# Transposes of probabilities and of v in two row halves of 64, with a PSUM bank for each half

## The chip, the cores and the metric

The kernel runs on one core of a Trainium2 chip. The metric is the time of one execution on the device in microseconds (us). The chip's engines go by these names: PE is TensorE's matrix product and PEld its loading of the stationary operand ("weights"), DVE is VectorE, ACT is ScalarE, POOL is GpSimd, SP is SyncE, which here only issues transfers. Each engine works through its own queue in order and waits on semaphores for the others. PSUM, into which PE writes, has eight banks of 512 fp32 values for each of 128 partitions.

## The reference

One decoder layer over 1024 prompt tokens and 8 x 4 decode tokens, all in fp32. What matters here is the sliding-window attention of the prompt, 8 heads of 64 on 2 key/value heads, in blocks of 128 queries that see their own block and the one before:

```python
def _sink_attention(q, k, v, mask, sinks):
    s = jnp.einsum('bnqhgd,bnkhd->bnhgqk', q, k) * (HEAD_DIM ** -0.5)
    s = jnp.where(mask, s, -jnp.inf)
    m = jnp.maximum(jnp.max(s, axis=-1, keepdims=True), sink)
    p = jnp.exp(s - m)
    denom = jnp.sum(p, axis=-1, keepdims=True) + jnp.exp(sink - m)
    return jnp.einsum('bnhgqk,bnkhd->bnqhgd', p / denom, v)
```

Around it stand an RMS norm and one input projection (q, k, v and a pooling branch), a pooling mixer, one output projection over both branches, a second norm, a SwiGLU network of width 2816, and a gated per-layer input:

```python
    x = x + _rms(mix, n_mix_post)
    f = _rms(x, n_ffn_pre)
    f = (silu(f @ w_gate) * (f @ w_up)) @ w_down
    x = x + _rms(f, n_ffn_post)
    x = x + sigmoid(x @ w_ple_gate) * (p @ w_ple)
```

## The kernel before, in words

Activations lie with the channels on the partitions and the 1056 tokens along the free dimension, in three groups of 352 tokens (`G`, `N`). Large products are made of a high and a low fp32r part for each operand, three matmuls for each chunk of 128 input channels (`gemm`, through the helper `mm`, L128). A weight tile arrives by DMA and is split in two: a cast on ACT (L173) gives the high part, a subtraction on DVE (L174) the low part.

Attention works on the eight blocks of 128 queries in the order 6, 7, 5, 0, 1, 2, 3, 4; in what follows "the second block" is the second in this order. For one block, `scores` multiplies q and k of both key/value heads in two row halves of the PE array (64 channels each) and merges the scores of the current and the previous block into one tile of 128 keys for each head: a key column that lies after the query belongs to the previous block. `weigh` makes the softmax: maxima, exponentials (ACT, L732), sums and reciprocals (DVE, L737 and L738), and a multiplication on POOL (L740). The rows of the tile are queries, its columns keys.

`turned` transposes the eight heads with PE, so that the keys lie on the partitions. A transpose is a matmul through the helper `mt` (L122): the data are the stationary operand, the identity is the moving one. Four heads go into one PSUM bank, and two multiplications by 0/1 masks on DVE take them out: `ptc` (L796) for the keys of the current block, `ptp` (L798) for those of the previous block. `values` multiplies with v in two query halves of 64, because the merged tile lets a half be served by `vmix`, in which rows 64 to 127 come from the block before:

```python
        for i, v in enumerate((vmix, vtok)):
            for kv, cols, hs in sides:
                mm(os_[i][cols, :256], v[:, b, cols], ptc[:, hs, q[i]], start=True, stop=False)
        for i in range(2):
            for kv, cols, hs in sides:
                mm(os_[i][cols, :256], vtok[q[i], b - 1, cols], ptp[q[i], hs, q[i]], start=False, stop=True)
```

`v_turned`, ahead of the eight blocks, transposes v in the same way; ACT copies it to `vtok` (L690), and POOL copies to `vmix` (L691, L692).

Between the steps of a block stand products of the output projection, which `filler` takes from a list (`out_pool`, `out_attn`, `out_proj`): the loop runs scores of the next block, one fill product, transposes, one fill product, values. PE's own order is the written one (`keep_in_program_order` in `mt` and `mm`). On the other engines a scheduler may reorder, except for the instructions that pass through `fix` while `fixed[0]` is set, which is so in the last block and in some other places.

After attention, `ffn_steps` begins with the RMS norm of the output projection (`rstd_steps`): sums over the partitions on PE, a square root on ACT (L395), a reciprocal on DVE (L396), two diagonal matrices on DVE (L402), and their product with a tile of ones on PE, which spreads the result over all partitions. Meanwhile `out_attn` goes on and adds its products to the sum in SBUF (L908).

Of the kernel before, what the change touches and what calls it, by code (L numbers as in the profile page):

```python
# [13 lines left out]
ALU = mybir.AluOpType  # L14
AX = mybir.AxisListType

P = 128
# [14 lines left out]
WIN = 128  # L32
NB = SEQ // WIN
# [5 lines left out]
REST = FFC - SLAB * NSLAB  # L39

AHEAD = 3

LOOK = 4
PLE = 256
# [18 lines left out]
def trunk_kernel(  # L63
# [33 lines left out]
    te, ve, se, ge = nc.tensor, nc.vector, nc.scalar, nc.gpsimd  # L97
# [10 lines left out]
    def nm(s):  # L108
        cnt[0] += 1
        return f"{s}{cnt[0]}"  # L110

    def act_tile(shape, dt=F32, s="a"):
        return apool.tile(shape, dt, tag="a", bufs=A_SLOTS, name=nm(s))
# [3 lines left out]

    pinned = [False]

    def mt(out, src):  # L120

        ins = te.transpose(out, src, ident)  # L122
        if pinned[0]:
            tc.keep_in_program_order(ins)

# [6 lines left out]
    def bank():  # L132
        return psum.tile([P, 512], F32, tag="b", name=nm("b"))
# [4 lines left out]
    def const(shape, src=None, s="c", dt=F32):  # L138
        t = cpool.tile(shape, dt, name=nm(s))
        if src is not None:  # L140
            nc.scalar.dma_start(t, src)
        return t
# [3 lines left out]
    ident = const([P, P])  # L146
# [20 lines left out]
    def fix(ins):  # L167

        if fixed[0]:
            tc.keep_in_program_order(ins)  # L170
# [75 lines left out]
    def step(kind, *args):  # L246
        STEPS.append((kind, args))

    def s_one(s, i):
        c = SLAB * s + i  # L250
        step("one", s, i, (direct_item(w_gu[c, 0]), direct_item(w_gu[c, 1])))
# [5 lines left out]
    def s_dn_one(s, *ts):  # L257
        for t in ts:
            step("dn_one", s, t, direct_item(w_dn[s, t // 2, t % 2]))
# [4 lines left out]
    def s_dn_rest(*gs):  # L264
        step("dn_rest", gs, [direct_item(w_dl[j], (P, REST, 512)) for j in range(2)])

    for s in range(AHEAD):
        for i in range(SLAB):
# [4 lines left out]
    for s in range(NSLAB):  # L273
        for i in range(SLAB):
            s_pair(s, i)
            if s == 0 and i < 2:
                s_dn_one(AHEAD - 1, 2 * i, 2 * i + 1)
                if i == 1:
# [8 lines left out]
    step("combine")  # L287
    for s in range(AHEAD, NSLAB):
        for i in range(SLAB):
            s_one(s, i)  # L290
            if s > AHEAD:
                s_dn_one(s - 1, i)
            if (s, i) == (AHEAD, 1):
                s_dn_rest(0, 1)
# [367 lines left out]
    kT, vT, qT = qkv[0], qkv[1], qkv[2:]  # L662
# [5 lines left out]
    qd, am, vdec = misc[:, 0, :], misc[:, 1:5, :], misc[: NDEC * DSEQ, 5, :]  # L668
# [12 lines left out]
    vtok, vmix = act_tile([P, NB, P]), act_tile([P, NB, P])  # L681

    def v_turned():
        for h in range(2):
            ps = bank()
            for i in range(4):
                b = 4 * h + i
                mt(ps[:, i * P : (i + 1) * P], vT[:, b * P : (b + 1) * P])
            v = ps.rearrange("p (b c) -> p b c", c=P)
            se.copy(vtok[:, 4 * h : 4 * h + 4, :], v)  # L690
            ge.tensor_copy(vmix[0:64, 4 * h : 4 * h + 4, :], vtok[0:64, 4 * h : 4 * h + 4, :])  # L691
        ge.tensor_copy(vmix[64:P, 1:NB, :], vtok[64:P, 0 : NB - 1, :])  # L692
        ps = bank()
        mt(ps[: NDEC * DSEQ, :P], vT[:, SEQ:])
        se.copy(vdec, ps[: NDEC * DSEQ, :P])
        nc.scalar.dma_start(kp_o, kT[:, SEQ - WIN : SEQ])
        nc.scalar.dma_start(vp_o, vtok[:, NB - 1, :])
# [44 lines left out]
    def m4(i):  # L742
        return am[:, i, :].unsqueeze(1).to_broadcast([P, 4, WIN])

    def v4(a):
        return a.rearrange("p (c k) -> p c k", k=WIN)

    def scores(b, now_=True):


        t = act_tile([P, 8, WIN])
        nk = 2 * WIN if b else WIN
        lo = b * WIN + WIN - nk
        at = WIN * 4 // nk
        both = [[bank() for _ in range(4 // at)] for _ in range(2)]
        for c in range(4):
            for kv in range(2):
                rows = slice(64 * kv, 64 * kv + 64)
                i = c % at
                mm(  # L760
                    both[kv][c // at][:, i * nk : (i + 1) * nk],
                    qT[c][rows, b * WIN : (b + 1) * WIN],
                    kT[rows, lo : lo + nk],
                    start=True,
                    stop=True,
                )
        for kv in range(2):
            tk = t[:, 4 * kv : 4 * kv + 4, :]
            for i, ps in enumerate(both[kv]):
                tc_ = tk[:, i * at : (i + 1) * at, :]  # L770
                v = ps.rearrange("p (c k) -> p c k", k=nk)
                if b:
                    m = am[:, 0, :].unsqueeze(1).to_broadcast([P, at, WIN])
                    se.copy(tc_, v[:, :, :WIN])
                    ve.copy_predicated(tc_, m.bitcast(mybir.dt.int32), v[:, :, WIN:])
                else:
                    ve.tensor_tensor(tc_, v, m4(1), op=ALU.add)
        if now_:
            weigh(t)
        return t  # L780
# [6 lines left out]
    def turned(b, t):  # L787

        ptc = act_tile([P, 8, WIN])
        ptp = act_tile([P, 8, WIN]) if b else None  # L790
        for kv in range(2):
            ps = bank()
            hs = slice(4 * kv, 4 * kv + 4)
            for c in range(4):
                mt(ps[:, c * P : (c + 1) * P], t[:, 4 * kv + c, :])
            fix(ve.tensor_tensor(ptc[:, hs, :], v4(ps), m4(2), op=ALU.mult))  # L796
            if b:
                fix(ve.tensor_tensor(ptp[:, hs, :], v4(ps), m4(3), op=ALU.mult))  # L798
        return ptc, ptp

    def values(b, parts):
# [132 lines left out]

    order = [6, 7, 5, 0, 1, 2, 3, 4]
    v_turned()
    fixed[0] = True
    td = dscores()
    fixed[0] = False
    t = scores(order[0], False)  # L940
# [15 lines left out]
    for a, b in zip(order, order[1:] + [None]):  # L956

        fixed[0] = lazy[0] = b is None
        t2 = ahead or (None if b is None else scores(b))
        ahead = None  # L960
        filler(1)
        parts = turned(a, t)
        if b is None:
            lazy[0] = False
            weights(WOA[1][0], 1)
        filler(1)
        values(a, parts)
        t = t2
# [251 lines left out]
    def do_one(s, i, items):  # L1220
        if (s, i) == (AHEAD, 0):
            do_reload_sums()
        sl = tmp(N, "sl")
        se.activation(sl, direct(need(items[0]), fs[2]), AF.Silu)
        ve.tensor_tensor(sl, sl, direct(need(items[1]), fs[2]), op=ALU.mult)
        hid_put(2, s, i, sl)
# [85 lines left out]
    def do_reload_sums():  # L1312
        os_[2] = [half(2, s="o") for _ in range(2)]
        for d, t in zip(osd, os_[2]):
            nc.sync.dma_start(t, d)
# [217 lines left out]
```

## Time and profile before

| | |
|---|---|
| median of 3 runs | 1080.22 us (1079.08 to 1080.45) |
| profiled execution | 1079.83 us, of which the span from its first to its last instruction is 1078.0 us |
| PE busy, PEld busy | 1071.1 us (99%), 1052.5 us (98%) |
| DVE, ACT, POOL busy | 874.9 us (81%), 510.7 us (47%), 277.4 us (26%) |
| granted TensorE clock | 1.0 |
| HBM | 113.86 MB read, 15.87 MB written |
| transposes of v | at 128.2 us of the span |
| transposes of the eight blocks | from 147.8 to 212.4 us |
| feed-forward and gated input | from about 216 us to the end |

All times in rows of the trace are counted from the start of the span. In a row of the time line stand the start, the time, the engine, the line, the operation, output<-input by the program's names, for PE the part of the array (rows * columns), the shape, and the count of like instructions that the row holds; its time then reaches from the start of the first to the end of the last. In brackets stands idle time ahead of it and what ended it. Matmuls are pipelined: the time of one includes its way through the array, so the distance of two starts tells what one costs. `128*128` uses the whole array; `64*128` means that two products stand in the row halves at the same time.

### The profile page before, as it was taken

To read this page: it belongs to the slowest core of one execution; us is meant where nothing else is said; L and a number is where in the kernel's file an instruction comes from. 1 tells how busy PE (TensorE), PEld (TensorE's weight loads), DVE (VectorE), ACT (ScalarE), POOL (GpSimd) and SP (SyncE) were. 2 spreads that over 40 slices of the span, in tenths; PEclk is the share of its full clock that TensorE was granted. 3 is DMA by queue.
4 is the path that set the end of the run, shared out by engine and by line. 5 is a ranking of instruction groups with operands and counts; after the bars stand their busy time and mean duration, and the time that the engine had idled before them with its cause. 6 is when DMAs were issued, how large, how long until landed. Compare 5 with 4: busy or idle time off the path is not lost. (4 is left out here: it accounts for less than half of the span.)

```text
span 1078.0 us, 17744 instructions
## 1 busy us (share of the span) xinstructions
PE 1071.1 (99%) x6883; PEld 1052.5 (98%) x6883; DVE 874.9 (81%) x1303; ACT 510.7 (47%) x872; POOL 277.4 (26%) x211
## 2 busy tenths in 40 slices
PE   9999999999999999999999999999999999999998
PEld 9999988899999999999999999999999999999998
DVE  6876378896979967796598898898899998969983
ACT  7423277664555533445543343343344365545441
POOL 0073022200000024445445444444452000023300
PEclk9999999999999999999999999999999999999999
DMA  8121311543544422322212212212234556454361
GB/s 299 59 73 40 104 53 40 201 152 135 215 165 137 138 98 78 135 76 79 89 70 82 92 62 90 87 59 98 79 113 167 176 176 248 157 212 151 107 207 61
DMA packets 43572, 130.88 MB, mean 121 GB/s; under 512 B 5060, under 2 KB 15716, under 8 KB 43488
## 3 DMA queue, kind: packets, MB, share of 16 engines
q1 hardware_dynamic: 42160, 127.98, 34.5%
q10 hardware_dynamic: 1328, 1.77, 0.5%
q8 instruction: 54, 0.88, 0.3%
q14 instruction: 30, 0.25, 0.1%
HBM read 113.86 MB, written 15.87 MB: 120 GB/s over the span
## 5 line engine op out<-in xcount | busy, mean ns | idle before, releaser
L1104 POOL TENSOR_TENSOR wr<-wr,wr 128x512 f32<-128x512 f32 x108 | 171.0, 1597 | 480.2 <-DMA wr<-in_w_gu_dram 257.0
L173 ACT CAST wh<-wr 128x1024 fp32r<-128x1024 f32 (+1 forms) x138 | 142.1, 1031 | 166.0 <-PE b L128 104.2
L174 DVE TENSOR_TENSOR wl<-wr,wh 128x1024 fp32r<-128x1024 f32 (+1 forms) x138 | 169.0, 1226 | 43.2 <-ACT wh L173 24.6
L128 PE MATMUL b<-fh,wh 128*128 128x352 f32 x624 | 201.7, 323 | 0.6 <-DVE p L1131 0.6
L128 PE MATMUL b<-fl,wh 128*128 128x352 f32 x624 | 199.8, 320 | 0.0
L128 PE MATMUL b<-fh,wl 128*128 128x352 f32 x624 | 199.7, 320 | 0.0
L173 ACT CAST sh<-wr 128x1024 fp32r<-128x1024 f32 x72 | 75.7, 1052 | 138.3 <-POOL wr L1104 123.1
L128 PE MATMUL b<-fh,sh 128*128 128x352 f32 x416 | 134.3, 323 | 0.0
L128 PE MATMUL b<-fl,sh 128*128 128x352 f32 x416 | 133.2, 320 | 0.0
L128 PE MATMUL b<-fh,sl 128*128 128x352 f32 x416 | 133.1, 320 | 0.0
L174 DVE TENSOR_TENSOR sl<-wr,sh 128x1024 fp32r<-128x1024 f32 x72 | 98.6, 1370 | 37.9 <-ACT sh L173 20.1
L128 PEld LDWEIGHTS b<-fh,wh 128*128 128x128 f32 x624 | 117.0, 187 | 1.3 <-DVE p L1131 0.9
L128 PEld LDWEIGHTS b<-fl,wh 128*128 128x128 f32 x624 | 117.2, 188 | 0.0
L128 PEld LDWEIGHTS b<-fh,wl 128*128 128x128 f32 x624 | 116.9, 187 | 0.0
L128 PE MATMUL b<-h,wh 128*128 128x352 f32 x480 | 105.8, 327 | 0.4 <-ACT h L449 0.4
L128 PE MATMUL b<-hid,wh 128*128 128x352 f32 x416 | 99.4, 322 | 0.0
L128 PEld LDWEIGHTS b<-h,wh 128*128 128x128 f32 x480 | 82.8, 191 | 1.5 <-ACT h L449 0.7
L1104 POOL TENSOR_TENSOR wr<-wr 128x512 f32<-128x512 f32 x36 | 50.9, 1415 | 106.7 <-DVE w L174 106.7
L128 PEld LDWEIGHTS b<-fl,sh 128*128 128x128 f32 x416 | 78.1, 188 | 0.0
L128 PEld LDWEIGHTS b<-fh,sh 128*128 128x128 f32 x416 | 78.0, 187 | 0.1
L128 PEld LDWEIGHTS b<-fh,sl 128*128 128x128 f32 x416 | 77.9, 187 | 0.0
L128 PE MATMUL b<-hp,sh 128*128 128x352 f32 x320 | 76.6, 322 | 0.2
(202 smaller groups left out, 2225.6 us busy)
## 6 DMA issues: line engine op xcount, KB each, us to landing
wr<-in_w_gu_dram SPq DMA_DIRECT2D x88, 512.0 KB, 3.3
wr<-in_w_dn_dram SPq DMA_DIRECT2D x40, 512.0 KB, 3.2
wr<-in_w_pg_dram SPq DMA_DIRECT2D x16, 512.0 KB, 3.6
x<-in_x_dram SPq DMA_DIRECT2D x6, 704.0 KB, 9.6
x1d<-x SPq DMA_DIRECT2D x6, 704.0 KB, 3.5
x<-x1d SPq DMA_DIRECT2D x6, 704.0 KB, 6.3
out_y_dram<-yo SPq DMA_DIRECT2D x24, 176.0 KB, 2.1
wr<-in_w_out_b_dram SPq DMA_DIRECT2D x8, 512.0 KB, 3.3
```

The source lines that it names most:

```text
L128: ins = te.matmul(*args, **kw)
L173: fix(se.copy(hi, src))
L174: fix(ve.tensor_tensor(lo, src, hi.bitcast(F32), op=ALU.subtract))
L1104: ge.tensor_tensor(out, a, b, op=op)
```

## The change

`mt` gets a range of rows. Each 128 x 128 transpose becomes two of 64 rows: the stationary operand is 64 partitions by 128 columns, the moving one the 64 x 64 corner of the identity, and the result, 64 columns wide, goes to one of two banks, one for each half. For a block, a bank now holds one query half of all eight heads, and not four heads with all queries. The masked copies go by query halves too; `ptp` is written only in the quadrants that `values` reads. The v transposes change in the same way. The transposes of the decode tokens stay as they are.

```diff
+HALVES = slice(0, 64), slice(64, P)
...
-    def mt(out, src):
-
-        ins = te.transpose(out, src, ident)
+    def mt(out, src, r=slice(0, P)):
+
+        ins = te.transpose(out, src[r], ident[r, r])
...
     def v_turned():
-        for h in range(2):
-            ps = bank()
-            for i in range(4):
-                b = 4 * h + i
-                mt(ps[:, i * P : (i + 1) * P], vT[:, b * P : (b + 1) * P])
-            v = ps.rearrange("p (b c) -> p b c", c=P)
-            se.copy(vtok[:, 4 * h : 4 * h + 4, :], v)
-            ge.tensor_copy(vmix[0:64, 4 * h : 4 * h + 4, :], vtok[0:64, 4 * h : 4 * h + 4, :])
+        both = [bank() for _ in range(2)]
+        for b in range(NB):
+            for ps, r in zip(both, HALVES):
+                mt(ps[:, 64 * b : 64 * b + 64], vT[:, b * P : (b + 1) * P], r)
+        for ps, r in zip(both, HALVES):
+            se.copy(vtok[:, :, r], ps.rearrange("p (b c) -> p b c", c=64))
+            ge.tensor_copy(vmix[0:64, :, r], vtok[0:64, :, r])
         ge.tensor_copy(vmix[64:P, 1:NB, :], vtok[64:P, 0 : NB - 1, :])
...
-        for kv in range(2):
-            ps = bank()
-            hs = slice(4 * kv, 4 * kv + 4)
-            for c in range(4):
-                mt(ps[:, c * P : (c + 1) * P], t[:, 4 * kv + c, :])
-            fix(ve.tensor_tensor(ptc[:, hs, :], v4(ps), m4(2), op=ALU.mult))
+        both = [bank() for _ in range(2)]
+        for c in range(8):
+            for ps, r in zip(both, HALVES):
+                mt(ps[:, 64 * c : 64 * c + 64], t[:, c, :], r)
+        for ps, r in zip(both, HALVES):
+            v = ps.rearrange("p (c k) -> p c k", k=64)
+            m = am[:, 2:4, r].unsqueeze(2).to_broadcast([P, 2, 8, 64])
+            fix(ve.tensor_tensor(ptc[:, :, r], v, m[:, 0], op=ALU.mult))
             if b:
-                fix(ve.tensor_tensor(ptp[:, hs, :], v4(ps), m4(3), op=ALU.mult))
+                fix(ve.tensor_tensor(ptp[r, :, r], v[r], m[r, 1], op=ALU.mult))
```

Because the scheduler places the other engines' instructions anew, the order on DVE and ACT changes in places. The line numbers of the changed kernel are 2 higher up to `v_turned` and differ by a few behind it.

On PE, at the first block: the transposes of the eight heads (tile `a`, identity `c_77`) between two fill products. Before:

```order
L128 MATMUL b_1560<-ml_730,wh_994 128x352
L128 MATMUL b_1560<-mh_729,wl_995 128x352
L122 MATMUL b_1576<-c_77,a_1350 128x128 x4
L122 MATMUL b_1583<-c_77,a_1350 128x128 x4
L128 MATMUL b_1590<-mh_734,wh_994 128x352
```

Now, up to the third of the eight pairs:

```order
L130 MATMUL b_1568<-mh_729,wl_995 128x352
L124 MATMUL b_1584<-c_77,a_1358 128x64
L124 MATMUL b_1585<-c_77,a_1358 128x64
L124 MATMUL b_1584<-c_77,a_1358 128x64
L124 MATMUL b_1585<-c_77,a_1358 128x64
L124 MATMUL b_1584<-c_77,a_1358 128x64
```

Eight transposes of 128 columns, four into each of two banks in turn, have become sixteen of 64 columns that alternate between two banks; the products around them stay.

On DVE, at the second block: `es`, `sm` and `nmx` belong to the softmax of the block after it, `wl<-wr,wh` is the weight split. Before:

```order
L725 TENSOR_TENSOR es_1643<-c_75,nmx_1641 128x4
L725 TENSOR_TENSOR es_1658<-c_75,nmx_1656 128x4
L796 TENSOR_TENSOR a_1683<-b_1685,a_1280 128x512
L798 TENSOR_TENSOR a_1684<-b_1685,a_1280 128x512
L796 TENSOR_TENSOR a_1683<-b_1692,a_1280 128x512
L798 TENSOR_TENSOR a_1684<-b_1692,a_1280 128x512
L737 TENSOR_TENSOR sm_1646<-sm_1646,es_1643 128x4
L174 TENSOR_TENSOR wl_1917<-wr_1885,wh_1916 128x1024
L738 RECIPROCAL sm_1646<-sm_1646 128x4
```

Now:

```order
L726 TENSOR_TENSOR es_1674<-c_75,nmx_1672 128x4
L176 TENSOR_TENSOR wl_1957<-wr_1917,wh_1956 128x1024
L796 TENSOR_TENSOR a_1699<-b_1701,a_1280 128x8x64
L738 TENSOR_TENSOR sm_1662<-sm_1662,es_1659 128x4
L798 TENSOR_TENSOR a_1700<-b_1701,a_1280 64x8x64
L739 RECIPROCAL sm_1662<-sm_1662 128x4
L796 TENSOR_TENSOR a_1699<-b_1702,a_1280 128x8x64
L798 TENSOR_TENSOR a_1700<-b_1702,a_1280 64x8x64
```

The weight split has moved from behind the four masked copies to ahead of them, and two small steps of the softmax stand between the copies.

On DVE, at the first RMS norm after attention: `dg` are the diagonal matrices, `y<-y,b` the additions of `out_attn`. Before:

```order
L396 RECIPROCAL sw_2489<-sw_2489 128x88
L908 TENSOR_TENSOR y_1286<-y_1286,b_2496 128x352
L397 CAST dg_2488<-sw_2489 128x88
L398 TENSOR_TENSOR dg_2488<-sw_2489,dg_2488 128x88
L402 TENSOR_TENSOR dg_2488<-c_77,dg_2488 128x352 x2
L908 TENSOR_TENSOR y_1285<-y_1285,b_2512 128x352
```

Now:

```order
L398 RECIPROCAL sw_2561<-sw_2561 128x88
L908 TENSOR_TENSOR y_1286<-y_1286,b_2568 128x352
L399 CAST dg_2560<-sw_2561 128x88
L908 TENSOR_TENSOR y_1285<-y_1285,b_2584 128x352
L400 TENSOR_TENSOR dg_2560<-sw_2561,dg_2560 128x88
L404 TENSOR_TENSOR dg_2560<-c_77,dg_2560 128x352 x2
```

The third addition has moved ahead of the diagonals. On PE the order is unchanged there: the product into `b_2512` (now `b_2584`) stands directly before the broadcast of `dg`.

More of the change, by code (lines that the diff above doesn't have):

```diff
@@ L743, in m4 @@
         return am[:, i, :].unsqueeze(1).to_broadcast([P, 4, WIN])
-    def v4(a):
-        return a.rearrange("p (c k) -> p c k", k=WIN)
     def scores(b, now_=True):
```

## The prediction

> **What bounds the kernel now.** I read the engine table first, then the chain that ended last, then the stretches of time, and then the attention stretch row by row: TensorE's matmuls (PE), its weight loads (PEld), and VectorE (DVE).
>
> ```profile
> PE 1071.1 (99%) x6883; PEld 1052.5 (98%) x6883; DVE 874.9 (81%) x1303; ACT 510.7 (47%) x872; POOL 277.4 (26%) x211
> 1018.34 55.58 PE b L128 x348
> 147.00:216.00 69.00, 69.00 (x511) 57.70 (x509) 58.11 (x150) 49.78 (x190) 15.81 (x14) 1.00 0.30 102
> ```
>
> PE is busy throughout, the chain's longest piece is PE alone, and in the third row (PE, PEld, DVE, ACT, POOL busy, granted clock) PE fills all 69 us of the attention stretch at full clock. So a slot saved on PE there, or a stall added, should reach the end one for one. A busy row contains the array's latency, so I count distances between starts.
>
> **What a transpose costs now.** The rows give start, time and shape; one group may be a whole run of instructions.
>
> ```profile
> 147.66 0.32 PE L128 MATMUL b<-mh,wl 128*128 128x352 f32 x1
> 147.82 1.03 PE L122 MATMUL b<-c,a 128*128 128x128 f32 x8
> 148.86 0.33 PE L128 MATMUL b<-ml,wh 128*128 128x352 f32 x1
> 137.86 0.82 PE L122 MATMUL b<-c,a 128*128 128x128 f32 x6
> L122 PEld LDWEIGHTS b<-c,a x79: 97/140/143, 128.1 to 212.3; 128*128 128x128 f32 x76, 128*32 128x32 f32 x3
> L122 PE MATMUL b<-c,a x79: 272/272/273, 128.2 to 212.4; 128*128 128x128 f32 x76, 128*32 128x128 f32 x3
> ```
>
> Eight transposes last 1.03 us of which the last is 0.272: (1.03 - 0.27)/7 = 0.109 us from start to start. Of the six at 137.86 the last two (decode tail, `t[:, kv, 256:]`) load only 32 columns, and the distance is the same: (0.82 - 0.27)/5 = 0.110. So the 128 moving columns set it, not the load: a half of 64 should stream in 0.055. The data are the stationary side. The loads took 97 ns for 32 columns and 140 for 128, that is 0.45 ns a column, 0.057 us for 128, and the halves still load 128 columns each.
>
> **What two row halves cost.** No transposes of this shape are in the trace; other products in row or column halves are, and so are the changes of the array's mode around them.
>
> ```profile
> 150.46 0.32 PE L128 MATMUL b<-mh,wl 128*128 128x352 f32 x1
> 150.71 0.63 PEld L128 LDWEIGHTS b<-a,a 128*64 128x64 f32 x8 [0.22 <-issue]
> 152.32 1.60 PEld L128 LDWEIGHTS b<-a,a 64*128 64x128 f32 x16 [0.39 <-issue]
> 153.72 0.60 PE L128 MATMUL b<-a,a 64*128 64x256 f32 x4
> 154.25 0.43 PE L128 MATMUL b<-mh,wh 128*128 128x352 f32 x1
> 154.51 0.32 PE L128 MATMUL b<-ml,wh 128*128 128x352 f32 x1
> 144.76 1.01 PEld L128 LDWEIGHTS b<-a,a 128*64 128x64 f32 x32 [0.17 <-issue]
> L128 PEld LDWEIGHTS b<-a,a 64*128 64x128 f32 x132 | 11.4, 186 | 4.3 <-issue 2.8 <-ACT a L732 0.4 <-DVE sm L738 0.2
> L128 PEld LDWEIGHTS b<-a,a 128*64 128x64 f32 x92 | 5.1, 136 | 2.8 <-issue 1.5 <-ACT es L729 0.2 <-ACT a L732 0.2
> ```
>
> The scores (64*128, two row halves) run side by side: 16 loads in 1.60, since each of the eight products goes through in two passes, each pass in pairs. The second pair of loads may follow the first after its 0.10, the other six distances are (1.60 - 0.19 - 0.10)/6 = 0.22, the time in which 256 columns stream, twice what 128 take above. A change of mode is paid in full. From the last whole-array product to the first load of the new mode it is 150.71 - 150.46 = 0.25 instead of the usual 0.16. On the way back, the last score pair starts 0.22 after 153.72, has streamed at 154.15, and the next product stands at 154.25: 0.10 of draining; its own load then delays the second product to 154.51, 0.26 later. At present the transposes run in the whole-array mode of their neighbours and pay none of this.
>
> Period of a pair: streaming alone gives 0.055; load and stream one after the other 0.057 + 0.055 = 0.112. The nearest row is the decode values at 144.76, which stream almost nothing and are held by loads: 16 pairs in 1.01, (1.01 - 0.14)/15 = 0.058 for loads of 64 columns, which by the two last rows cost (186 - 136)/64 = 0.78 ns a column or 0.050: load plus about 0.005. So I take 0.060, with 0.055 and 0.112 as ends.
>
> One block, counted from the start of the last product before it. Before: the second product behind stands at 148.86 - 147.66 = 1.20. After: first load 0.25, streaming from 0.31, last pair 7 x 0.060 later at 0.73, streamed at 0.785, drained at 0.885, second product at 1.145. Saving 0.05; with the ends +0.09 and -0.31. Eight blocks: **-0.4 us** (-0.7 to +2.5).
>
> ```profile
> 128.06 0.32 PE L128 MATMUL b<-h,wl 128*128 128x352 f32 x1
> 129.29 0.18 PEld L128 LDWEIGHTS b<-a,a 64*32 64x32 f32 x16 [0.21 <-issue]
> ```
>
> For v the distance is now 1.23, with nine transposes and one change of mode. After: 0.885 as above, then the 32 decode tokens in the whole-array mode (0.01 + 0.11) and another drain of 0.095: 1.10. **-0.13 us** (-0.17 to +0.25). The copies of v on ACT and POOL keep counts and sizes; the first values product is 21 us later, which covers their later start.
>
> **Masked copies.** Per block the four DVE copies read the same 512 elements a partition, from two banks, so I count their time as unchanged. They start later (all 16 transposes before the first, not four) but are needed less soon: the first values product used both heads' copies, so three of the four; now it needs one, the second query half the third. That removes a wait that shows in two blocks:
>
> ```profile
> 166.75 0.82 PEld L128 LDWEIGHTS b<-a,a 128*64 128x64 f32 x8 [0.22 <-issue]
> 167.96 0.21 PEld L128 LDWEIGHTS b<-a,a 64*64 64x64 f32 x8 [0.39 <-issue]
> 197.52 0.74 PEld L128 LDWEIGHTS b<-a,a 128*64 128x64 f32 x8 [0.22 <-issue]
> 198.64 0.21 PEld L128 LDWEIGHTS b<-a,a 64*64 64x64 f32 x8 [0.39 <-issue]
> ```
>
> There the first part of values takes 1.21 and 1.12, elsewhere 1.02 (159.15 to 160.17 below): **-0.3 us** (0 to -0.3).
>
> **Two steps that the scheduler moves.** The order on DVE changes at two places, and both hold up PE. The first is the second block of eight (PE transposes at 156.26). A weight split, which stood behind the four masked copies, now stands before them, and it waits for its cast on ACT.
>
> ```profile
> 156.30 1.05 ACT L173 CAST wh<-wr 128x1024 fp32r<-128x1024 f32 x1 [1.31 <-PE b L128]
> 157.01 0.69 DVE L796 TENSOR_TENSOR a<-b,a 128x512 f32<-128x512 f32 x1
> 157.61 0.68 DVE L798 TENSOR_TENSOR a<-b,a 128x512 f32<-128x512 f32 x1
> 159.40 0.15 DVE L737 TENSOR_TENSOR sm<-sm,es 128x4 f32<-128x4 f32 x1
> 159.47 1.22 DVE L174 TENSOR_TENSOR wl<-wr,wh 128x1024 fp32r<-128x1024 f32 x1
> 160.60 0.17 DVE L738 RECIPROCAL sm<-sm 128x4 f32<-128x4 f32 x1
> 159.15 0.63 PEld L128 LDWEIGHTS b<-a,a 128*64 128x64 f32 x8 [0.22 <-ACT es L729]
> 160.17 0.21 PEld L128 LDWEIGHTS b<-a,a 64*64 64x64 f32 x8 [0.39 <-issue]
> ```
>
> By then PE is 0.18 ahead (v and one block), and the cast, which PE releases, with it: done at 157.17. The split starts at 157.2 and lets the next instruction in 1.13 later (159.47 to 160.60): first copy 158.34. A copy occupies 0.60 (157.01 to 157.61), and one small softmax instruction of 0.07 (159.40 to 159.47) now stands behind each of the first two: third copy at 159.68, done at 160.36. PE reaches the values at 159.15 - 0.23 = 158.92 and would stream the second query half (load 0.05, two passes of 0.22) at 159.41; now it loads after 160.36, streaming at 160.45. **+1.05 us** (0 to +1.2). The fourth copy ends at 160.96, when PE has just drained. The same swap occurs in the fifth block, where the fill product between transposes and values has 24 matmuls, not 12, which covers the 1.13.
>
> The second place is the first RMS norm after attention. Its broadcast on PE needs the two diagonal products on DVE (L402). Ahead of these now stands the addition that reads the product just before the broadcast.
>
> ```profile
> 224.18 0.32 PE L128 MATMUL b<-mh,wl 128*128 128x352 f32 x1
> 224.34 0.57 PE L128 MATMUL b<-dg,c 128*128 128x352 f32 x2
> 224.75 0.33 PE L128 MATMUL b<-mh,wh 128*128 128x352 f32 x1
> 223.30 0.25 DVE L398 TENSOR_TENSOR dg<-sw,dg 128x88 fp32r<-128x88 f32 x1
> 223.47 0.95 DVE L402 TENSOR_TENSOR dg<-c,dg 128x352 fp32r<-128x352 f32 x2
> 224.54 0.52 DVE L908 TENSOR_TENSOR y<-y,b 128x352 f32<-128x352 f32 x1
> 224.98 1.61 DVE L1016 TENSOR_TENSOR y<-y,b 128x1408 f32<-128x1408 f32 x1
> ```
>
> Before, the diagonals were ready at 224.42, just in time for the second broadcast product near 224.50. Now the addition cannot start before 224.54, when its product has left the array. The next instruction (L398) follows at 224.98, the diagonals 0.17 later and 0.95 long: 226.10. The second broadcast product starts at 226.15 instead of 224.50: **+1.65 us** (0 to +1.8), and since PE works in order, everything behind waits. Other swaps (score copies against the decode softmax, casts, squares) stand where nothing on PE waits; I cost them at nothing, their cover being the products between.
>
> Sum: -0.4 - 0.13 - 0.3 + 1.05 + 1.65 = +1.9 us. The profiled execution took 1079.83 (span 1078.0), so 1081.7; the median of the runs is 0.39 higher: **1082.1 us**.
>
> **A rule against the change.** The Trainium skill, "TensorE: Matmul & The Clock Gate", section "LDWEIGHTS (loading the stationary operand)", says that a load's time goes by its columns alone, 1/1.2 ns each, whatever the rows: 107 ns for 128. By that a half costs as much load as a whole and pairs come no faster than 107 ns: the first rival's time. The trace agrees for ordinary loads (0.78 ns a column) but not for those of transposes (0.45).
>
> **The rivals.**
> - Loads hold the pairs, or do not overlap streaming: period 0.11, from the row of ordinary 128-column loads or from the serial end. Then a block ends at 1.51 to 1.56, +0.31 to +0.36, eight +2.5 to +2.9; v +0.25; with the two stalls and the wait removed +5.2 to +5.6: **1085.6**. Against it: 32 and 128 loaded columns gave the same 0.109, so loads do lie beside streaming. It decides once the period passes 0.065. Chance 0.13.
> - The stalls do not come, because the copies or diagonals are ready sooner than reckoned: -0.4 - 0.13 - 0.3 = -0.8: **1079.4**. Against it: DVE and PE each work in order, and both waits follow from the order. Chance 0.13.
> - The change of mode costs nothing around transposes: a block saves 8 x (0.109 - 0.060) = 0.39, eight 3.1, v 0.4. With the stalls 1079.2, without them **1076.4**. Against it: every change in the rows above shows the drain. Chance 0.04.
>
> **Chances and range.** My forecast holds 0.70, within 0.7 us. A change under 0.2%, here 2.16 us, is about what a measurement of this kernel cannot tell from none: the line lies at 1082.38, inside the forecast's spread, so I put 0.42 of the 0.70 below it and 0.28 above. Above too: the first rival. Below: the second and the third with stalls. Faster: the third without stalls and a little of the second, 0.04. Slower 0.41, same 0.55. The range 1079.3 to 1084.8 holds the forecast, half of the second rival, and a pair period up to 0.09.
>
> **What would show it.** Transposes: 16 per block, 7 starts of pairs 0.060 apart, loads near 140 ns, second product behind at 1.145. Values: the second block's first part 2.0 us instead of 1.02, the two others at 1.02. Broadcast: `b<-dg,c` ending 1.6 us later behind L908. Wrong it would be by loads of 187 ns or pairs 0.11 apart, by masked copies slower than 0.7 us, or by a gap at one of the two places that stays under 0.3 us.

## The result, and the profile after

| | before | after |
|---|---|---|
| median of 9 runs each | 1079.42 us (1078.10 to 1080.45) | 1082.66 us (1081.09 to 1084.05) |
| profiled execution, its span | 1079.83 us, 1078.0 us | 1082.22 us, 1080.4 us |

The ratio of the runs is 1.0023, with a 95% interval of 1.0014 to 1.0031: slower by 1.5 to 3.3 us. The two profiled executions are 2.39 us apart. The clock was granted in full in both. First the engines of the kernel after, then the attention stretch and the one behind it (columns as before: the stretch, its length, PE, PEld, DVE, ACT and POOL busy, granted clock, DMA share, GB/s).

```profile
PE 1070.5 (99%) x6955; PEld 1047.4 (97%) x6955; DVE 876.5 (81%) x1303; ACT 510.5 (47%) x872; POOL 277.5 (26%) x211
```

```profile
147.00:216.00 69.00, 67.99 (x563) 54.13 (x561) 57.51 (x146) 48.70 (x188) 14.81 (x14) 1.00 0.30 102
216.00:230.00 14.00, 12.70 (x88) 11.26 (x85) 10.57 (x16) 8.52 (x14) 0.00 (x0) 1.00 0.34 115
```

PE no longer fills the attention stretch: 1.0 us of it is empty, and 1.3 us of the stretch behind; before, PE was busy for all of both (69.00 and 14.00 us). Next the time line of PE and PEld around the transposes of v and of the first block, and the group of all transposing loads (minimum, median and maximum in ns, forms). In the kernel after, L130 is the product and L124 the transpose.

```profile
127.59 0.32 PE L130 MATMUL b<-h,wl 128*128 128x352 f32 x1
128.69 0.66 PE L130 MATMUL b<-a,a 64*32 64x256 f32 x16
...
147.07 0.32 PE L130 MATMUL b<-mh,wl 128*128 128x352 f32 x1
147.32 0.71 PE L124 MATMUL b<-c,a 64*128 64x64 f32 x16
147.96 0.43 PE L130 MATMUL b<-mh,wh 128*128 128x352 f32 x1
148.22 0.32 PE L130 MATMUL b<-ml,wh 128*128 128x352 f32 x1
147.32 0.57 PEld L124 LDWEIGHTS b<-c,a 64*128 64x128 f32 x16 [0.22 <-issue]
```

```profile
L124 PEld LDWEIGHTS b<-c,a x151: 93/138/140, 127.8 to 212.9; 64*128 64x128 f32 x144, 128*128 128x128 f32 x4, 128*32 128x32 f32 x3
```

Sixteen transposes last 0.71 us of which the last is 0.22, so eight pairs start within 0.49: the first distance is 0.111, the other six are 0.060 to 0.063. The second product behind stands 148.22 - 147.07 = 1.15 us after the last one ahead, where it was 1.20. At v the decode scores follow 128.69 - 127.59 = 1.10 us after the last product, where it was 1.23.

Then the loads of the values products (PEld) in the first, second, third and fourth block, with the idle time ahead of them in brackets (0.22 and 0.39 are the usual ones):

```profile
151.08 0.20 PEld L130 LDWEIGHTS b<-a,a 64*64 64x64 f32 x4 [0.39 <-issue]
151.51 0.19 PEld L130 LDWEIGHTS b<-a,a 64*64 64x64 f32 x4 [0.23 <-DVE a L798]
159.10 0.23 PEld L130 LDWEIGHTS b<-a,a 128*64 128x64 f32 x4 [0.44 <-ACT es L730]
160.42 0.23 PEld L130 LDWEIGHTS b<-a,a 128*64 128x64 f32 x4 [1.09 <-ACT a L733]
161.03 0.25 PEld L130 LDWEIGHTS b<-a,a 64*64 64x64 f32 x8 [0.39 <-issue]
168.15 0.20 PEld L130 LDWEIGHTS b<-a,a 128*64 128x64 f32 x4 [0.34 <-DVE a L796]
178.44 0.23 PEld L130 LDWEIGHTS b<-a,a 128*64 128x64 f32 x4 [0.41 <-issue]
```

In the second block the second query half loads at 160.42, 1.32 after the first, and the first itself stands 0.23 later than the usual 0.25 after the last product at 158.62: here is the stall of the weight split. But the first, third and fourth block wait too, which the prediction did not have. VectorE (DVE) shows why; first the first block before, then the first, with a row of POOL, the second and the third after (sums L737 and now L738, masked copies L796 and L798, split L176).

```profile
150.42 0.66 DVE L798 TENSOR_TENSOR a<-b,a 128x512 f32<-128x512 f32 x1
151.00 0.73 DVE L737 TENSOR_TENSOR sm<-sm,es 128x4 f32<-128x4 f32 x1
```

```profile
150.00 0.72 DVE L738 TENSOR_TENSOR sm<-sm,es 128x4 f32<-128x4 f32 x1
149.67 1.04 POOL L741 TENSOR_TENSOR a<-a,sm 128x512 f32<-128x512 f32 x1 [5.44 <-DVE sm L739]
150.76 0.69 DVE L798 TENSOR_TENSOR a<-b,a 64x512 f32<-64x512 f32 x1
...
157.16 1.22 DVE L176 TENSOR_TENSOR wl<-wr,wh 128x1024 fp32r<-128x1024 f32 x1 [0.30 <-ACT wh L175]
158.30 0.68 DVE L796 TENSOR_TENSOR a<-b,a 128x512 f32<-128x512 f32 x1
159.65 0.65 DVE L796 TENSOR_TENSOR a<-b,a 128x512 f32<-128x512 f32 x1
...
167.33 0.16 DVE L738 TENSOR_TENSOR sm<-sm,es 128x4 f32<-128x4 f32 x1 [0.42 <-ACT es L730]
167.41 0.68 DVE L796 TENSOR_TENSOR a<-b,a 128x512 f32<-128x512 f32 x1
```

In the first block a softmax sum that elsewhere takes 0.15 us lasts 0.72, and the fourth masked copy now stands behind it, where it stood ahead. The sum is not waiting for ACT: the exponentials that it adds were done at 149.80. It ends at 150.73, 0.02 us after POOL's multiplication (149.67 to 150.71), and before it did the same (its end at 151.73, POOL's at 151.72), only behind the copy, where it cost nothing; the last section has more on this. In the third block the third copy stands behind a sum that does wait for an exponential on ACT, 0.42 us. The second block is as predicted: split at 157.16, first copy 158.30, third 159.65. Last the broadcast of the norm:

```profile
225.33 0.52 DVE L908 TENSOR_TENSOR y<-y,b 128x352 f32<-128x352 f32 x1 [1.27 <-PE b L130]
225.77 0.24 DVE L400 TENSOR_TENSOR dg<-sw,dg 128x88 fp32r<-128x88 f32 x1
225.93 0.95 DVE L404 TENSOR_TENSOR dg<-c,dg 128x352 fp32r<-128x352 f32 x2
226.59 0.77 PE L130 MATMUL b<-dg,c 128*128 128x352 f32 x2 [1.30 <-DVE dg L404]
```

DVE is idle for 1.27 us until PE's product is there, then adds, and only then makes the diagonals, for which PE waits 1.30 and a little more between the two broadcast products.

PE's order, without the transposes, is the same in both kernels, so each product's start can be set against the start of the same product in the profile of before. The table gives this shift in us at five places: ahead of v, behind v, behind attention, behind the broadcast, and near the end. The first four experiments stand in it too; each row is one profiled execution.

| kernel | 125 us | 130 us | 223 us | 230 us | 1060 us |
|---|---|---|---|---|---|
| after | -0.47 | -0.60 | +0.79 | +2.46 | +2.39 |
| both orders restored | +0.49 | +0.36 | -0.38 | -0.35 | -1.08 |
| diagonals alone | -0.04 | -0.17 | +1.23 | +1.25 | +1.10 |
| before, ordered | -0.43 | -0.43 | -0.64 | -0.61 | -0.63 |
| before, swapped | +0.33 | +0.33 | +1.57 | +3.21 | +3.63 |

The first column belongs to no change: up to there PE and DVE have the same order in all, and over all kernels profiled here the shift lies between -0.47 and +0.73. So the change costs 2.39 + 0.47 = 2.86 us from 125 us on; the runs' interval holds it as well as the 2.39 between the spans.

### The profile page after: what moved, and what is told of

It reads as the page before. It is cut to its first block, busy times and chain, and to the rows that moved or that the text cites. A ratio compares the mean times of both kernels' runs of the same rounds, so it can differ in the third digit from the quotient of the medians.

```text
span 1080.4 us, 17886 instructions
## 1 busy us (share of the span) xinstructions
PE 1070.5 (99%) x6955; PEld 1047.4 (97%) x6955; DVE 876.5 (81%) x1303; ACT 510.5 (47%) x872; POOL 277.5 (26%) x211
## 5 line engine op out<-in xcount | busy, mean ns | idle before, releaser
L176 DVE TENSOR_TENSOR wl<-wr,wh 128x1024 fp32r<-128x1024 f32 (+1 forms) x138 | 169.2, 1228 | 43.3 <-ACT wh L175 25.5
L130 PE MATMUL b<-fh,wh 128*128 128x352 f32 x624 | 201.7, 323 | 0.6 <-DVE p L1131 0.6
L130 PE MATMUL b<-fl,wh 128*128 128x352 f32 x624 | 199.9, 320 | 0.0
L130 PE MATMUL b<-fh,wl 128*128 128x352 f32 x624 | 199.7, 320 | 0.0
L130 PE MATMUL b<-fh,sh 128*128 128x352 f32 x416 | 134.3, 323 | 0.0
L130 PE MATMUL b<-fl,sh 128*128 128x352 f32 x416 | 133.2, 320 | 0.0
L130 PE MATMUL b<-fh,sl 128*128 128x352 f32 x416 | 133.1, 320 | 0.0
L176 DVE TENSOR_TENSOR sl<-wr,sh 128x1024 fp32r<-128x1024 f32 x72 | 97.6, 1356 | 38.4 <-ACT sh L175 23.8
L130 PEld LDWEIGHTS b<-fh,wh 128*128 128x128 f32 x624 | 117.0, 187 | 1.3 <-DVE p L1131 0.9
L130 PEld LDWEIGHTS b<-fl,wh 128*128 128x128 f32 x624 | 117.2, 188 | 0.0
L130 PEld LDWEIGHTS b<-fh,wl 128*128 128x128 f32 x624 | 116.9, 187 | 0.0
L130 PE MATMUL b<-h,wh 128*128 128x352 f32 x480 | 104.9, 324 | 0.8 <-ACT h L451 0.6
L130 PE MATMUL b<-hid,wh 128*128 128x352 f32 x416 | 99.4, 322 | 0.0
L130 PEld LDWEIGHTS b<-h,wh 128*128 128x128 f32 x480 | 81.4, 188 | 2.3 <-DVE h L453 1.0
L130 PEld LDWEIGHTS b<-fl,sh 128*128 128x128 f32 x416 | 78.1, 188 | 0.0
L130 PEld LDWEIGHTS b<-fh,sh 128*128 128x128 f32 x416 | 78.0, 188 | 0.1
L130 PEld LDWEIGHTS b<-fh,sl 128*128 128x128 f32 x416 | 77.9, 187 | 0.0
L130 PE MATMUL b<-hp,sh 128*128 128x352 f32 x320 | 76.6, 322 | 0.1
```

The lines of the kernel that those rows point to most:

```text
L130: ins = te.matmul(*args, **kw)
L176: fix(ve.tensor_tensor(lo, src, hi.bitcast(F32), op=ALU.subtract))
```

## Experiments

### The orders on VectorE, restored and forced

The first experiment keeps the halves and rules DVE's order: sums of the next softmax, weight splits and additions of the fill product behind a block's last masked copy, the third addition behind the diagonals.

```diff
+        with tc.issue_after(last_copy[0].ins):   # DVE: behind the last masked copy
+            for f in late_sums:                  # sums, reciprocals of weigh()
+                f()
+            late_sums.clear()
+            filler(1)
...
+        if (m, g) == (1, 0):
+            with tc.issue_after(last_dg[0].ins): # DVE: behind the second diagonal
+                ve.tensor_tensor(yv, yv, ps[:, : NS[g]], op=ALU.add)
```

> The changed kernel with VectorE's order restored: the four masked copies of a block come ahead of the sums of the next block's softmax and of weight splits, and at the first RMS norm the diagonals come ahead of the third addition. Theory (the loss is VectorE's order; the halves themselves save): 0.13 us at v, eight times 0.045 at the transposes and the waits of the values product, so about 0.9 us less than the kernel before; the second block's first part of values back at 1.02 us, the broadcast no later than its product ahead. Rival (the halves cost it themselves, by changes of mode, narrower copies or the bank for each half): the loss of about 2.9 us against the kernel before stays, and the waits in values with it.

Measured: 1078.94 us against 1080.12 for the kernel before, ratio 0.9991 (0.9983 to 1.0000). Against the changed kernel's 1.0023 that is 3.5 us. In the table the stretch from 125 to 223 us now gains 0.86 us, and the broadcast adds nothing. The second block's values are back to their old form:

```profile
159.41 0.63 PEld L130 LDWEIGHTS b<-a,a 128*64 128x64 f32 x8 [0.22 <-ACT es L734]
160.42 0.21 PEld L130 LDWEIGHTS b<-a,a 64*64 64x64 f32 x8 [0.39 <-issue]
223.96 0.57 PE L130 MATMUL b<-dg,c 128*128 128x352 f32 x2
```

So the theory holds: on balance the halves cost nothing themselves, VectorE's order cost all of it and more. Of the shift of -1.08 us at the end some 0.9 belongs to something else, told at the end of this document.

The second experiment orders the diagonals alone (the second part of the diff).

> The changed kernel, only the diagonals ahead of the third addition. Theory: 1.7 us less than the changed kernel, so about 1.2 us more than the kernel before; waits in values stay. Rival (the wait at the broadcast is only moved, as the next norm steps or the additions come later): under 0.5 us less than the changed kernel.

Measured: 1081.60 us, ratio 1.0010 (1.0002 to 1.0019), 1.4 us less than the changed kernel by the ratios. The table shows +1.27 in attention as in the changed kernel (+1.26), and +0.02 at the broadcast instead of +1.67.

The third applies the first one's rules to the kernel before.

> The kernel before, whole transposes, with the same rule for VectorE: masked copies ahead of sums and splits, diagonals ahead of the third addition. Theory: there the order stood right already but for one sum at 197 us, so within 0.3 us of the kernel before, most likely 0.1 less. Rival (the rule helps any layout, so the halves save nothing of their own): as fast as the changed kernel with the same rule, about 0.9 us less than before.

Measured: 1079.64 us, ratio 0.9996 (0.9987 to 1.0005). From 125 to 223 us it gains 0.21, a quarter of what the halves gain with the same rules. The rest, 0.65, comes with the halves, by one profiled execution of each; the ratios alone (0.9991 and 0.9996) are too close to tell.

The fourth forces the two predicted swaps on the kernel before, which transposes whole tiles.

```diff
+        if (m, g) == (1, 0):       # DVE: diagonals behind this addition
+            for late in last_low:
+                behind(late, add)
...
+        if a == 0:                 # DVE: second block's copies behind this split
+            behind(firsts[order[1]], splits[35])
```

> The kernel before, whole transposes, with the two swaps forced on VectorE: the weight split ahead of the second block's masked copies, the third addition ahead of the diagonals. Theory: 1.7 us at the broadcast and 1.1 to 1.3 in the second block's values, so about 2.9 us more than the kernel before, as much as the changed kernel loses, without any half. Rival (the halves cost it): no change, within 0.5 us.

Measured: 1082.99 us, ratio 1.0027 (1.0016 to 1.0038): as slow as the changed kernel, without a single half. The waits are the same ones at the same places:

```profile
159.65 0.19 PEld L128 LDWEIGHTS b<-a,a 128*64 128x64 f32 x2 [0.39 <-ACT es L739]
160.92 0.62 PEld L128 LDWEIGHTS b<-a,a 128*64 128x64 f32 x6 [1.08 <-DVE a L806]
227.28 0.86 PE L128 MATMUL b<-dg,c 128*128 128x352 f32 x2 [1.21 <-DVE dg L412]
```

+1.25 in attention and +1.64 at the broadcast, 2.89 in all where 2.9 was expected. Within attention the second block lost 1.44, more than the 1.1 to 1.3 expected, and the third gave 0.19 back. For the two predicted swaps this and the first experiment settle the cause from both sides. That the total equals the changed kernel's is partly chance: there the other waits (+0.57) and the savings of the halves (-0.48) nearly cancel. Those other waits were only taken away, by the first experiment, and not forced.

### Whether two halves run side by side

```diff
-        for c in range(8):
-            for ps, r in zip(both, HALVES):
+        for ps, r in zip(both, HALVES):
+            for c in range(8):
                 mt(ps[:, 64 * c : 64 * c + 64], t[:, c, :], r)
```

> The changed kernel with VectorE's order restored, but the eight transposes of the first row half come first and then the eight of the second, so that no two of different halves alternate. Theory (two row halves run side by side, each transpose takes 0.058 for its load and streaming): sixteen steps of 0.058 instead of eight, 0.47 us more in each of eight blocks, 3.7 us more than the version with the order restored. Rival (the pair's 0.058 is two loads of 0.029 one after the other, so order is nothing): no change.

Measured: 1081.92 us, ratio 1.0025 (1.0015 to 1.0035), 3.7 us above the version with the order restored by the ratios, which is the number that the theory gave. The rows divide it differently:

```profile
148.53 1.01 PE L124 MATMUL b<-c,a 64*128 64x64 f32 x16
149.47 0.43 PE L130 MATMUL b<-mh,wh 128*128 128x352 f32 x1
```

Sixteen transposes take 1.01 instead of 0.71, so a block costs 0.30 more, not 0.47: the second half's first transpose starts at 148.83, while the first half still has three to go. In eight blocks this is 2.4 us, and so much shows between 125 and 223 us (+1.49, where the version with the order restored has -0.86). The rest of the 3.7 belongs elsewhere: in the two profiled executions it arises behind 1000 us, where the waits told at the end differ. Two halves do run side by side, but the 0.47 was too large. It also shows a half alone: its third to fifth start at 148.70, 148.76 and 148.82, 0.061 apart, as far as pairs are. The load and the streaming are therefore not paid one after the other even within one half. The Trainium skill, "TensorE: Matmul & The Clock Gate", section "Part 3: Packing small matmuls — row/col tiling", says that a load overlaps running matmuls only when their row groups differ; with the prediction's 0.057 for a load and 0.055 for streaming that would be 0.112 within a half, and these transposes do not show it.

### Sharing the array's mode with the scores

A block's transposes pay for the change of mode: 0.25 us to the first load, the first load itself, and 0.10 of draining. The scores run in the same row halves, so a version with the transposes directly behind the scores might beat both kernels. At v the decode tail is now transposed ahead of the halves.

```diff
         t2 = ahead or (None if b is None else scores(b))
-        filler(1)
-        parts = turned(a, t)
+        if a != order[0] and b is not None:
+            parts = turned(a, t)
+            filler(1)
+        else:
+            filler(1)
+            parts = turned(a, t)
```

> The changed kernel with VectorE's order restored; in blocks two to seven the half transposes stand directly behind the next block's scores, which use the same row halves, and the fill product goes behind them; at v the decode tail is transposed ahead of the halves. Theory of the mode change: a block's transposes now add 0.84 us to PE (1.156 from the last product ahead to the second behind, less two slots of 0.16), of which only the streaming, 8 x 0.058 = 0.47, should be left next to the scores: 0.33 less in each of six blocks and 0.2 at v, 2.2 in all. But the softmax of the block has one fill product less time: by the version with the order restored, POOL's last multiplication would end 0.5 to 1.5 us behind the scores in four of the blocks, some 3.5 us of waits, so between 0 and 1.5 us more than that version. Rival (softmax comes sooner too, since the masked copies come sooner): 2 us less than that version, about 3 us less than the kernel before.

Measured: 1080.13 us against 1079.59 for the kernel before, ratio 1.0005 (0.9996 to 1.0015): no gain, and by the ratios 1.5 us more than the version with the order restored, the far end of what was expected. The waits say why:

```profile
PE b L124 <- POOL a L746: 2.1, 3, 1.1
PE b L130 <- DVE p L1155: 0.9, 1, 0.9
```

Three blocks' transposes waited 2.1 us for POOL's multiplication (the second row is the wait near the end of the kernel, told in the last section). So in the next one the scores run two blocks ahead (`scores(order[i + 2])` directly ahead of `turned(a, ts[i])`, both fill products behind it).

> As the one with the transposes next to the scores, but the scores run two blocks ahead, so that the softmax has a whole round: in blocks one to six scores, half transposes, two fill products, values. Theory: no wait for POOL, six blocks at 0.3 to 0.37 us and 0.2 at v: 2 us less than the version with the order restored, 3 us less than the kernel before. Rival (the drain is paid between scores and transposes as well, because the array's mode is not shared): no more than 0.5 us less than the version with the order restored. Rival (one more tile in use at a time makes scores wait for a slot): waits of ACT's copies and a time at or above the kernel before.

Measured: 1080.39 us, ratio 1.0003 (0.9993 to 1.0013). The same with whole transposes:

> The kernel before, whole transposes and the same rule for VectorE, with the scores two blocks ahead and the transposes directly behind the scores. Whole transposes use the whole array, so the mode changes are as many as before. Theory: within 0.5 us of the kernel before. Rival (the place itself brings the gain, by waits that go): as fast as the halves next to the scores, about 3 us less than before.

Measured: 1080.18 us, ratio 1.0007 (0.9999 to 1.0016). First the halves, then the whole transposes behind the scores of the first block:

```profile
147.88 0.66 PE L124 MATMUL b<-c,a 64*128 64x64 f32 x16
148.47 0.43 PE L130 MATMUL b<-mh,wh 128*128 128x352 f32 x1
```

```profile
147.82 1.09 PE L122 MATMUL b<-c,a 128*128 128x128 f32 x8
148.67 0.41 PE L128 MATMUL b<-mh,wh 128*128 128x352 f32 x1
```

From the first score product (146.05 and 145.90) to the fill product the halves take 2.42 us and the whole transposes 2.77. Next to the scores the halves thus save 0.35 in a block, where between fill products they save 0.04; the sharing of the mode was reckoned at 0.33. At v the decode tail ahead of the halves brought 0.10, not 0.2 (1.00 instead of 1.10). But in the version with halves PE waited again, in the second block's values for 1.2 us (as did the version with whole transposes), and in two blocks' transposes:

```profile
PE b L130 <- DVE a L806: 1.0, 1, 1.0
PE b L124 <- POOL a L746: 0.5, 1, 0.5
PE b L124 <- ACT sq L910: 0.4, 1, 0.4
```

DVE had put sums behind steps of a later block, and a maximum ahead of the copies. Ruling that order too (copies, then sums, then the later block's maxima, then splits), with halves and with whole transposes:

> As the one with the scores two blocks ahead, but VectorE's order is ruled there as well: masked copies, then the sums of the next block's softmax, then the maxima of the block after it, and every weight split behind the copies. There 0.8 and 0.9 us were lost in two blocks' transposes (the softmax's sums stood behind steps of the block after it) and 1.4 us in the values of two blocks (sums and a maximum ahead of the copies), 3.2 us in all. Theory: with these gone the shared mode shows, 2 us less than the version with only the order restored and about 3 us less than the kernel before. Rival (other waits take their place, as VectorE has no more room in this stretch): within 1 us of the kernel before.

> The same program with whole transposes. Theory: no transposes in halves, so no shared mode; within 0.6 us of the kernel before, and 2 to 3 us more than the same program with halves. Rival (the order and place bring the gain, not the halves): as fast as the halves.

Measured: 1094.72 us, ratio 1.0135 (1.0118 to 1.0152), and 1091.43 us, ratio 1.0110 (1.0091 to 1.0130). Both theories fell. In the first, the values ran without a wait now, but fill products and one block's transposes did not:

```profile
PE b L130 <- DVE wl L176: 3.5, 2, 2.1
PE b L130 <- DVE ml L715: 3.4, 2, 3.3
PE b L124 <- ACT sq L911: 2.7, 1, 2.7
```

They waited for weight splits and for the subtraction that takes the values out of PSUM (`ml`), the transposes for ACT. That whole transposes lose nearly as much shows that it is the rule and not the halves. Not all of the loss is waits. The granted clock, 1.00 throughout attention in the kernel before, was 0.93 here on average:

```profile
147.00:216.00 69.00, 58.33 (x457) 49.13 (x454) 51.65 (x133) 44.32 (x179) 12.72 (x12) 0.93 0.16 56
```

Three times it was 0.50 for some 3.4 us, from 167.7, 201.8 and 208.6, each less than 1 us behind the end of one of PE's waits (3.3, 2.7 and 2.1 us). Products that follow one another every 0.16 us came every 0.29 there, so by an estimate each of the three cost about 1.5 us. The version with whole transposes had one such stretch. Taking splits and fill products out of the rule:

> As the one with the scores two blocks ahead and VectorE's order ruled, but without the rule that holds the weight splits and the fill products' additions behind the masked copies; there fill products waited for splits and casts, some 15 us in all. Theory (that rule was the loss): the fill products run as in the version with the order restored, so 2 us less than it and 3 us less than the kernel before. Rival (the maxima held behind the sums make the loss): still over 8 us more than the kernel before.

Measured: 1090.55 us, ratio 1.0101 (1.0087 to 1.0115), still over 8 us, as the rival had it. The splits were a part, but `mh` and `ml` were still waited for, 3.4 and 2.6 us, and the clock was at 0.50 twice. Which of the remaining rules does it was not followed further.

The last one puts transposes next to the scores only in the three blocks that had not waited for POOL (`if a in (7, 1, 3)` in the first diff of this section).

> As the one with the half transposes next to the scores, but only in the blocks whose transposes did not wait for POOL there (the second, the fifth and the seventh); the others stand between fill products as in the changed kernel, and VectorE's order is restored. Theory: 0.33 us less in each of the three blocks and 0.2 at v, so 1.2 us less than the version with the order restored and about 2 us less than the kernel before. Rival (the softmax of the following block is late for it, since its sums stand behind the copies): waits of about 1 us in a block behind, and no gain.

Measured: 1080.07 us, ratio 1.0005 (0.9996 to 1.0014). The rival was right. The second block gained what the shared mode promised (scores to values 6.43 us, 6.78 in the version with the order restored), but then the third block's values waited 0.5 us for a masked copy and a later block's transposes as long for POOL, among others:

```profile
PE b L124 <- POOL a L746: 0.5, 1, 0.5
PE b L130 <- DVE a L806: 0.5, 1, 0.5
```

So of all versions with halves only the one with both orders restored came out at or below the kernel before, and by less than a measurement can tell.

## Why the prediction was right, and where it was not

- **Total.** 1082.1 was predicted and 1082.66 measured. By its own steps the sum was +1.9; the same steps measure -0.35 - 0.13 + 0.57 + 1.19 + 1.67 = +2.95 (by the table 2.93 at 230 us), of which 0.07 came back by 1060 us. In the profiled execution an earlier start of 0.47 hid part of it. That the time came within 0.6 us is partly luck: the sum was added to a median of 1080.22 from three runs, and nine runs of the kernel before have 1079.42, so this start was 0.8 too high and the sum 1.0 too low.
- **Block transposes, -0.4.** Right: 0.061 from pair to pair (0.060 taken), second product at 1.156 instead of 1.145, since the first distance is 0.111. Eight blocks: -0.35. The rival by which loads hold the pairs 0.11 apart is excluded: the loads took 138 ns, as before, with half the rows. The Trainium skill's rule, "TensorE: Matmul & The Clock Gate", section "LDWEIGHTS (loading the stationary operand)", gives 107 ns for 128 columns; as an estimate it would have set 107 ns a pair, and these came at 61.
- **v, -0.13.** Right, 1.234 to 1.106.
- **Second block's split, +1.05.** Right: 0.26 ahead of the values, 0.89 in their first part, 0.04 in their second, together +1.19. The chip's first copy stood at 158.30 (158.34 reckoned), the third at 159.65 (159.68); the size differs because even the first values product had to wait.
- **Broadcast, +1.65.** Right, +1.67. The second rival (no stalls) falls with these two.
- **Masked copies, -0.3.** Wrong, +0.57. The step that failed is the sentence that the other swaps "stand where nothing on PE waits". In the first block a sum moved ahead of the fourth copy, which the last of the values products needs: their second part took 1.007 instead of 0.592 (+0.41), since that sum ended only when POOL's multiplication did. In the third a sum moved ahead of the third copy: both parts took 1.932, before 1.801 (+0.13), where 1.61 was expected. In the sixth the wait went as predicted (-0.11). In the fourth block, which has no block before it and multiplies all queries at once, the first product needs both query halves, where before it needed one group of heads, and in both kernels a sum that waits for ACT stands ahead of the second copy: +0.14, which goes when the sums are ordered behind the copies (first experiment: 1.26 us from the last product ahead to the end of the values, after 1.49 and before 1.35). I had counted which copies a product needs, but not what the queue puts between them.
- **Third rival.** Changes of mode for nothing are excluded by the 0.15 from the last pair to the product at 147.96, of which 0.06 is streaming, and by the 0.35 that sharing the mode saved in the second block (6.78 to 6.43).

## What to carry to other kernels

When a scheduler places instructions, a change on one engine is priced mostly by what it reorders on another: list every instruction that has moved ahead of one that the busiest engine waits for, small ones too, and ask of each what it waits for itself and what runs on POOL beside it. A sum of 0.15 us that another engine holds up for 0.6 costs as much as a long one, and such a hold shows as a longer row, not as idle time. A saving of 0.35 us in a place is only kept if the work that feeds that place has the time to spare; five versions here moved the transposes to a cheaper place and gave the gain back as waits.

## What the runs showed that was not expected

Near the end, an instruction on DVE and one on POOL overlap, and which of them is held differs from kernel to kernel. First the kernel before (DVE's addition, POOL's, and from the waits PE's), then the one with both orders restored:

```profile
1009.14 1.61 DVE L1399 TENSOR_TENSOR yo<-p,xm 128x352 f32<-128x352 f32 x1
1008.14 2.24 POOL L1104 TENSOR_TENSOR wr<-wr,wr 128x512 f32<-128x512 f32 x1 [9.25 <-DMA wr<-in_w_pg_dram]
```

```profile
PE b L128 <- DVE p L1131: 0.6, 1, 0.6
```

```profile
1008.97 0.52 DVE L1419 TENSOR_TENSOR yo<-p,xm 128x352 f32<-128x352 f32 x1
1007.86 3.39 POOL L1124 TENSOR_TENSOR wr<-wr,wr 128x512 f32<-128x512 f32 x1 [9.14 <-DMA wr<-in_w_pg_dram]
```

Either DVE's 0.52 becomes 1.61 while POOL's, which usually takes 1.30, takes 2.24, or POOL's takes 3.39. In the first case PE waits 0.6 us for DVE at 1018 us, in the second it does not; before and after both had the first, so it cancels between them. The Trainium skill, "Trainium Architecture — The Big Picture", section "What this means for kernel authors", calls the port that DVE and POOL share an exclusive lock and not a split of bandwidth, and these rows agree. What decides which side is held here is not shown: POOL's instruction started 0.75 to 1.55 us ahead of DVE's in the executions where DVE was held, and 0.90 to 1.11 ahead where POOL was. No experiment was made on it.

The same overlap lies behind the first block's stall. In all profiled executions together, 35 softmax sums between 126 and 216 us lasted longer than 0.2 us, and every one of them ended 0.02 us behind a multiplication of POOL; of the 197 that took less, only two overlapped one. By these rows a step of the softmax on POOL, released by the first sum and its reciprocal, holds the second sum, and with it the masked copy that now stands behind.
